# A hybrid streaming-encoder layer on one core: gates in order, a product moved, x on another queue, new planned transfer times

## The chip, the cores and the metric

One core of a Trainium2 chip runs the whole layer. The time is the device time of one execution, in microseconds (us). The engines are TensorE (PE; PEld are its weight loads), VectorE (DVE), ScalarE (ACT), GpSimd (POOL) and SyncE (SP), which only issues transfers. ScalarE and GpSimd issue transfers too.

## The reference, cut to what matters

```python
def hybrid_layer(x, norm_g, w_in, b_f, b_gate, qk_norm_g, rel_bias, w_up, w_out):
    b, s, _ = x.shape                                   # 1, 512, 2048
    hn = rmsnorm(x, norm_g)
    proj = jnp.einsum('bsd,dc->bsc', hn, w_in)
    br = proj[..., :QKVG_COLS].reshape(b, s, N_BRANCH, 4, BRANCH_W)
    f_logit = proj[..., QKVG_COLS:QKVG_COLS + N_HEADS] + b_f
    gates = jax.nn.sigmoid(proj[..., QKVG_COLS + N_HEADS:] + b_gate).reshape(b, s, N_BRANCH, D_MODEL)
    qa = rmsnorm(to_heads(br[:, :, 0, 0]), qk_norm_g[0])
    ...
    ya = forgetting_attention(qa, ka, to_heads(br[:, :, 0, 2]), f_logit)     # A: bias from a cumulative sum
    ...
    yb = chunked_relpos_attention(qb, kb, to_heads(br[:, :, 1, 2]), rel_bias) # B: learned relative bias
    yc = stick_breaking_attention(to_heads(br[:, :, 2, 0]), to_heads(br[:, :, 2, 1]),
                                  to_heads(br[:, :, 2, 2]))                   # C
    ys = jnp.stack([from_heads(ya), from_heads(yb), from_heads(yc)], axis=2)
    ys = ys * jax.nn.silu(br[:, :, :, 3])
    up = jnp.einsum('bsnw,nwd->bsnd', ys, w_up)
    merged = jnp.sum(gates * up, axis=2)
    return x + jnp.einsum('bsd,de->bse', merged, w_out)
```

Three branches of four heads of width 128 each; 512 tokens, all in float32. Nearly all of the arithmetic is in three products: the input projection (2048 to 12,292 columns), the up-projection of each branch (512 to 2048) and the output projection (2048 to 2048).

## The kernel before, in words

**Precision.** Every float32 operand is split into a high part and a rest, both in fp32r: hi is a copy by ScalarE, the rest a subtraction by VectorE. A product then takes three matmuls: hi x hi, hi x rest and rest x hi. For weights these are the tiles raw (as it lands), wh (L366, ScalarE) and wl (L371, VectorE). All matmuls of the large products stand on one helper line, L265. Eight raw buffers, three wh and two wl rotate.

**Work units.** The stream of work on TensorE is a list, units. A unit is one raw tile of weights, 128 x 1024, and twelve matmuls of 512 columns; its wh and wl are prepared two units ahead. The input projection and the output projection are cut by Strassen's scheme into tasks of seven products of four units each, (p, c) with p = 1 to 7 and c = 0 to 3. Products 1, 2 and 4 need one block of weights, a plain load by SyncE (L277). Products 5 and 7 need the sum of two blocks: a plain load, and then an accumulating transfer issued by GpSimd (L281) when the first has landed. Products 6 and 3 take 5's raw tile, to which VectorE adds the raw tile of 1 and then of 2 (L574). The results of a task are collected by Strassen.after: 5 and 1 are copied from their accumulators by ScalarE (L643), 6 and the others are added by VectorE (L652 on). There are four accumulators acc and four banks att for attention, transposes and, in one task, product 6.

**Stages.** First x is scaled and split while its sixteen blocks land (prep_x, L434 to L445); 42 matmuls on an identity matrix run on TensorE before the first real one (L417). Then twelve tasks, one per head: the C heads, the B heads, the A heads; the merge-gate logits gl and the branch inputs y are stored in memory and loaded again. The attention of a head is laid between the units of the next task. Then 24 units of the up-projection in twelve groups, (g, b) for four column groups g and three branches b: a group fills four accumulators, one for each of four token blocks tb, and VectorE multiplies each by a gate tile sg (L1251), to which ScalarE has applied the sigmoid (L1235, gates_of). From merged come the transposed operands m, their differences and splits (L256, L250), and then two output tasks, out_task(0) and out_task(1), whose results get x added and are stored.

**What sets the order.** The order of TensorE, ScalarE and VectorE is fixed while the kernel is written, by a planner (class Flow). Every piece of work is a generator that yields what it needs: an event, a buffer from a Slots pool, or an engine with a cost in us and a due time. Flow.run takes the piece that can start earliest by its own clocks, and among those the one due first. It reckons with planned landing times: landing for plain loads, add_up for accumulating ones, both on a common line. On the chip, the instructions of an engine run in the planned order, each waiting on what it really needs. SyncE's and GpSimd's queues follow the order in which the planner reaches the loads.

```python
    PLAIN = [(p, c) for p in (5, 1, 6, 7, 4, 2, 3) for c in range(CH)]
```

is the usual order of products.

## Time and profile before

| what | before |
|---|---|
| median of 3 runs | 1318.59 us (1318.33 to 1319.23) |
| the profiled execution | 1318.87 us, span 1317.2 us |
| TensorE busy | 1306.8 us, 99% of the span |
| VectorE, ScalarE, GpSimd busy | 1023.2, 751.5, 91.2 us |
| read and written | 266.03 MB, mean 202 GB/s |

In a timeline row stand the start, the length, the engine, the line, the operation, output and input, how many alike are joined in the row and, in brackets, how long the engine was idle ahead of it and what it waited for. In the chain of waits stand only the start, the length and what ran or was waited for. The row of a window begins with its length and the busy time of TensorE; in parentheses stand the numbers of instructions. The granted clock is 1.00 in all the stretches used.

### The profile page before, as it was taken

Reading aid. Unit: us, or ns where it says so; the run is one execution under the profiler, and the core shown is the slowest. Engines: PE = TensorE matmul, PEld = TensorE weight load, DVE = VectorE, ACT = ScalarE, POOL = GpSimd, SP = SyncE. Lnnn points to the kernel's source line nnn. Section 1 sums busy time; section 2 is a strip of 40 time slices with the busy share of each in tenths; the row PEclk is TensorE's granted clock in tenths of the full one; section 3 lists DMA queues with packets and bytes.
Section 4 is the critical chain, followed back from the end, with each engine's and each line's share of the span. In section 5 each row is a group of like instructions: output and inputs, shape, how many; then the busy total and the mean of one; then the engine's idle time right before and its main releaser. Section 6 shows DMA issues by size and latency. Waiting matters only on the chain.

```text
span 1317.2 us, 17191 instructions
## 1 busy us (share of the span) xinstructions
PE 1306.8 (99%) x6034; PEld 1078.7 (82%) x6034; DVE 1023.2 (78%) x1420; ACT 751.5 (57%) x1271; POOL 91.2 (7%) x115
## 2 busy tenths in 40 slices
PE   9999999999999999999999999999999999999998
PEld 7788888888888888888888888888887788878787
DVE  5877787887878777687776877778789668798667
ACT  7655464564557656566466654667568555454342
POOL 0000001110011100111011110110000000000110
PEclk9999999999999999999999999999999999999999
DMA  9755677866778757777577775777776656648883
GB/s 358 218 139 147 182 209 190 231 176 178 207 196 231 197 166 232 176 225 205 170 226 176 224 208 168 224 176 224 220 250 197 235 192 208 161 97 249 245 240 128
DMA packets 89063, 266.03 MB, mean 202 GB/s; under 512 B 11264, under 2 KB 11264, under 8 KB 88976
## 3 DMA queue, kind: packets, MB, share of 16 engines
q1 hardware_dynamic: 71552, 206.16, 46.5%
q0 software_dynamic: 14976, 54.53, 23.1%
q10 hardware_dynamic: 2448, 4.24, 0.8%
q8 instruction: 47, 0.77, 0.2%
q14 instruction: 40, 0.33, 0.1%
HBM read 245.19 MB, written 19.70 MB: 201 GB/s over the span
## 4 chain that ended last, share of the span: by engine, by line
PE 96%; DMA 2%; DVE 1%; ACT 1%; issue 0%; SPq 0%; ACTq 0%; POOLq 0%; DVEq 0%
PE acc L265 89%; DMA raw<-in_w_out 2%; PE att L801 1%; PE att L926 1%; PE att L260 1%; PE att L261 1%; PE att L262 1%; PE att L1016 1%; PE att L1015 1%; PE att L1285 1%; PE att L1014 1%; PE att L265 1%; ACT sg L1235 0%; DVE wl L371 0%; PE att L1118 0%; DMA x<-in_xT 0%
## 5 line engine op out<-in xcount | busy, mean ns | idle before, releaser
L371 DVE TENSOR_TENSOR wl<-raw,wh 128x1024 fp32r<-128x1024 f32 (+1 forms) x405 | 493.5, 1220 | 208.1 <-PE acc L265 116.1
L366 ACT ACTIVATE wh<-raw 128x1024 fp32r<-128x1024 f32 (+1 forms) x405 | 426.0, 1054 | 365.8 <-PE acc L265 276.3
L265 PE MATMUL acc<-wh,x 128*128 128x512 f32 x1664 | 429.8, 392 | 0.1
L265 PEld LDWEIGHTS acc<-wh,x 128*128 128x128 f32 x1664 | 308.7, 188 | 64.7 <-ACT t L246 0.9
L265 PE MATMUL acc<-wh,t 128*128 128x512 f32 x1056 | 272.6, 391 | 0.0
L265 PE MATMUL acc<-wl,x 128*128 128x512 f32 x832 | 229.8, 390 | 0.0
L265 PEld LDWEIGHTS acc<-wh,t 128*128 128x128 f32 x1056 | 196.7, 188 | 40.2
L265 PEld LDWEIGHTS acc<-wl,x 128*128 128x128 f32 x832 | 155.9, 188 | 33.1 <-DVE wl L371 0.4
L265 PE MATMUL acc<-wl,t 128*128 128x512 f32 x528 | 149.3, 390 | 0.0
L281 POOL DMA_DIRECT2D raw<-in_w_col x88 | 76.0, 864 | 877.5 <-ACT wh L366 195.3
L574 DVE TENSOR_TENSOR raw<-raw,raw 128x1024 f32<-128x1024 f32 x104 | 126.7, 1218 | 0.0
L265 PEld LDWEIGHTS acc<-wl,t 128*128 128x128 f32 x528 | 98.4, 188 | 19.6
L265 PE MATMUL acc<-wh,m 128*128 128x512 f32 x416 | 105.1, 390 | 1.9 <-ACT wh L366 1.9
L265 PE MATMUL acc<-wh,y 128*128 128x512 f32 x384 | 103.7, 391 | 1.3 <-DVE sg L1251 1.3
L265 PEld LDWEIGHTS acc<-wh,m 128*128 128x128 f32 x416 | 77.9, 188 | 18.8 <-ACT wh L366 2.7
L265 PEld LDWEIGHTS acc<-wh,y 128*128 128x128 f32 x384 | 71.7, 188 | 16.8 <-DVE sg L1251 2.2
L265 PE MATMUL acc<-wl,y 128*128 128x512 f32 x192 | 59.7, 391 | 0.0
L265 PE MATMUL acc<-wl,m 128*128 128x512 f32 x208 | 58.1, 390 | 0.1
L246 ACT ACTIVATE ah<-att 128x512 fp32r<-128x512 f32 (+3 forms) x48 | 21.0, 437 | 48.2 <-PE att L926 48.2
L265 PEld LDWEIGHTS acc<-wl,m 128*128 128x128 f32 x208 | 38.9, 188 | 8.5 <-DVE wl L371 0.5
L250 DVE TENSOR_TENSOR al<-att,ah 128x512 fp32r<-128x512 f32 (+3 forms) x48 | 23.5, 489 | 25.5 <-ACT ah L246 24.8
L265 PEld LDWEIGHTS acc<-wl,y 128*128 128x128 f32 x192 | 35.7, 188 | 7.2
(179 smaller groups left out, 1114.3 us busy)
## 6 DMA issues: line engine op xcount, KB each, us to landing
raw<-in_w_col SPq DMA_DIRECT2D x235, 512.0 KB, 4.6
raw<-in_w_col POOLq DMA_DIRECT2D x88, 512.0 KB, 7.9
raw<-in_w_out SPq DMA_DIRECT2D x40, 512.0 KB, 3.9
raw<-in_w_up SPq DMA_DIRECT2D x24, 512.0 KB, 3.6
sg<-gl SPq DMA_DIRECT2D x48, 256.0 KB, 4.6
raw<-in_w_out POOLq DMA_DIRECT2D x16, 512.0 KB, 6.2
gl<-u SPq DMA_DIRECT2D x22, 256.0 KB, 9.8
gl<-s SPq DMA_DIRECT2D x22, 256.0 KB, 5.2
```

What stands on the lines that cost most here:

```text
L246: nc.scalar.activation(hi, src, AF.Copy)
L250: nc.vector.tensor_sub(lo, src, f(hi))
L260: nc.tensor.matmul(ps, lh, rh, start=start, stop=False, skip_group_check=more)
L261: nc.tensor.matmul(ps, lh, rl, start=False, stop=False, skip_group_check=more)
L262: nc.tensor.matmul(ps, ll, rh, start=False, stop=stop, skip_group_check=more)
L265: nc.tensor.matmul(ps, w, x, start=start, stop=stop, skip_group_check=more)
L281: nc.gpsimd.dma_start(to, src, accum_op=ALU.add)
L366: nc.scalar.activation(u.hi, u.raw, AF.Copy)
L371: nc.vector.tensor_sub(u.lo, u.raw, f(u.hi))
L574: nc.vector.tensor_add(to.raw, to.raw, self.raw)
L801: nc.tensor.transpose(ps[:, blk(tb)], self.c[tb][:, blk(r)], identf)
L926: nc.tensor.transpose(ps[:, blk(i)], self.p[i][:, blk(j)], identf)
```

## The change

Seven parts:

1. The warm-up has 36 matmuls in place of 42, on a tile of ones that VectorE sets first, in a bank of its own. It no longer uses the identity, which GpSimd and VectorE make.
2. The planner's time of an accumulating transfer: it takes 250 KB/us of the common line, does not hold the line until its first half has landed, and lands 6.5 us later (it took 170 KB/us, waited, and landed 2.5 us later).
3. The constants are loaded by SyncE, ahead of everything, in place of ScalarE's queue; the first block of x is loaded by ScalarE's queue in place of SyncE's third place. The planner's clock begins at 4.0 in place of 5.0.
4. Buffers for wl are taken in the order of the units. The first unit's wh is made by VectorE, not ScalarE.
5. The first four blocks of x, not the first two, take the path that scales and copies in one ScalarE instruction; their plain scaling is due at 24.0.
6. The gates of the first group (g = 0, b = 0) are all asked for at one unit, so that they come ahead of the gates of later groups.
7. out_task(0) takes products 5 and 1 for all four columns before 6 (6 came after each pair of columns), and 6 uses acc banks. out_task(1) begins with product 1, then 5.

```diff
--- before.py
+++ after.py
@@ -29,7 +29,7 @@
 HS = S // 2
 EPS = 1e-6
 NEG = -1e30
-WARM = 42
+WARM = 36
 SCALE = HD ** -0.5
 LA = 2
 
@@ -279,8 +279,8 @@
 
     def add_up(to, src, ready, kb):
         nc.gpsimd.dma_start(to, src, accum_op=ALU.add)
-        line[1] = max(line[1], ready + 1.0) + kb / 170.0
-        return Event(line[1] + 2.5)
+        line[1] += kb / 250.0
+        return Event(max(line[1], ready) + 6.5)
 
     def stored(slots, n, kb):
 
@@ -289,12 +289,16 @@
 
     nc.scalar.preload_act_table_set("natural_log_exp_and_others")
     small_in = cp.tile([P, consts.shape[1]], F32, name="small_in")
-    nc.scalar.dma_start(small_in, consts)
+    nc.sync.dma_start(small_in, consts)
+    x_first = tp.tile([P, S], F32, tag="t2", name=nm("x"))
+    nc.scalar.dma_start(x_first, xT[0])
     gn = small_in[:, 0:KT]
     gqk = small_in[:, KT:KT + 4]
     bfc = small_in[:, KT + 4:KT + 5]
     wf = small_in[:, KT + 5:].rearrange("p (k h) -> p k h", h=NH)
 
+    oneb = cp.tile([P, P], BF16, name="oneb")
+    nc.vector.memset(oneb, 1.0)
     epsc = cp.tile([P, 1], F32, name="epsc")
     nc.gpsimd.memset(epsc, EPS)
     nhepsc = cp.tile([P, 1], F32, name="nhepsc")
@@ -343,6 +347,7 @@
 
 
         def __init__(self, mms, after=None, shape=(2, S), srcs=()):
+            self.took, self.prev = Event(), None
             self.shape, self.mms, self.after, self.srcs = list(shape), mms, after, srcs
             self.ready_hi, self.ready, self.there, self.raw = Event(), Event(), Event(), None
 
@@ -362,10 +367,17 @@
         n = u.shape[0] * S
         u.hi = wp.tile([P] + u.shape, F32R, tag="wh", name=nm("wh"), bufs=LA + 1)
         yield u.there
-        yield ACT, act_us(n)
-        nc.scalar.activation(u.hi, u.raw, AF.Copy)
+        if u is units[0]:
+            yield DVE, dve_us(n)
+            nc.vector.tensor_copy(u.hi, u.raw)
+        else:
+            yield ACT, act_us(n)
+            nc.scalar.activation(u.hi, u.raw, AF.Copy)
         set_(u.ready_hi)
+        if u.prev is not None:
+            yield u.prev.took
         yield wls, 1
+        set_(u.took)
         u.lo = wp.tile([P] + u.shape, F32R, tag="wl", name=nm("wl"), bufs=LA)
         yield DVE, dve_us(n)
         nc.vector.tensor_sub(u.lo, u.raw, f(u.hi))
@@ -413,8 +425,9 @@
     first_ps = att()
     atts.free.pop()
     nc.vector.memset(first_ps, 0.0)
+    early_ps = att()
     for _ in range(WARM):
-        nc.tensor.matmul(first_ps[:, :P], identb, identb, start=True, stop=True)
+        nc.tensor.matmul(early_ps[:, :P], oneb, oneb, start=True, stop=True)
     xps.free.clear()
 
 
@@ -428,15 +441,17 @@
         due = (5.0 + 3.2 * kt,)
         yield x_in[kt]
         x = xraw[kt]
-        if kt < 2:
+        if kt < 4:
             g = gn[:, kt:kt + 1]
             yield (ACT, act_us(S), *due)
             nc.scalar.activation(xs[kt].hi, two(x), AF.Copy, scale=g)
             set_(raw_hi[kt])
+            if kt == 0:
+                yield units[0].ready_hi
             yield (DVE, dve_us(S), *due)
             nc.vector.scalar_tensor_tensor(xs[kt].lo, two(x), g, f(xs[kt].hi), op0=ALU.mult, op1=ALU.subtract)
             set_(raw_ev[kt])
-            yield (DVE, 0.5, due[0] + 5.0)
+            yield (DVE, 0.5, 24.0)
             nc.vector.tensor_scalar_mul(x, x, g)
             set_(scaled[kt])
             return
@@ -1348,7 +1363,7 @@
     for g in (0, 2, 1, 3):
         for b in range(NB):
             for tb in range(QB):
-                at(len(units) - 3 + tb // 2, lambda n=(C, B, A)[b], g=g, tb=tb: gates_of(n, g, tb))
+                at(len(units) - (3 - tb // 2 if g or b else 2), lambda n=(C, B, A)[b], g=g, tb=tb: gates_of(n, g, tb))
             units.extend(up_units(g, b))
         for i in range(QB):
             at(len(units) - 1, lambda g=g, i=i: turned_m(g, i))
@@ -1376,11 +1391,10 @@
         def src(m, half, c):
             return w_out[2 * i + m, CH * half + c]
 
-        order, other = PLAIN, ()
+        order, other = PLAIN[CH:2 * CH] + PLAIN[:CH] + PLAIN[2 * CH:], ()
         if i == 0:
-            order = [(p, c) for cs in ((0, 1), (2, 3)) for p in (5, 1, 6) for c in cs]
-            order += PLAIN[3 * CH:]
-            other = (6,)
+            order = [(p, c) for cs in ((0, 1), (2, 3)) for p in (5, 1) for c in cs]
+            order += PLAIN[2 * CH:]
         return Strassen(src, mops, done, order, other, rest).units
 
     for i in range(2):
@@ -1390,6 +1404,9 @@
     def loads():
         def x(kt):
             yield t2s, 1
+            if kt == 0:
+                xraw[0], x_in[0].t = x_first, 3.6
+                return
             xraw[kt] = t2("x")
             x_in[kt].t = fetch(xraw[kt], xT[kt], 0.0, 256).t
 
@@ -1412,6 +1429,9 @@
         for u in units[9:]:
             yield from u.load()
 
+    for u, v in zip(units, units[1:]):
+        v.prev = u
+
     def stream():
         for i, u in enumerate(units):
             for g, slack in side.pop(i, ()):
@@ -1426,7 +1446,7 @@
                 spawn(u.after(), 0.0, flow.fin)
 
     line[0] = 0.8
-    flow.fin = 5.0
+    flow.fin = 4.0
     spawn(loads(), 0.0, 0.0)
     for kt in range(KT):
         spawn(prep_x(kt), 5.0)
```

Three places where the planned order moves.

**SyncE, then VectorE, at the first up-projection group.** sg is a gate tile, gl the logits in memory; in the rows of before, sg_9142 and sg_9167 are the gates of token blocks 0 and 1 of the first group, sg_9123 and sg_9125 of blocks 2 and 3. SyncE before:

```order
L277 DMA sg_9123<-gl_6773 128x512
L277 DMA sg_9125<-gl_6794 128x512
L277 DMA sg_9127<-gl_3786 128x512
L277 DMA sg_9129<-gl_3813 128x512
L277 DMA sg_9131<-gl_3889 128x512
L277 DMA sg_9133<-gl_3910 128x512
L277 DMA sg_9137<-gl_1042 128x512
L277 DMA sg_9139<-gl_1052 128x512
L277 DMA sg_9142<-gl_6670 128x512
L277 DMA raw_9148<-in_w_up 128x1024
L277 DMA sg_9167<-gl_6697 128x512
```

and with the change:

```order
L277 DMA sg_9120<-gl_6667 128x512
L277 DMA sg_9122<-gl_6694 128x512
L277 DMA sg_9124<-gl_6770 128x512
L277 DMA sg_9126<-gl_6791 128x512
L277 DMA sg_9128<-gl_3783 128x512
```

VectorE before:

```order
L1023 TENSOR_TENSOR y_8961<-y_8961,att_9116 128x512
L1251 TENSOR_TENSOR sg_9123<-acc_9087,sg_9123 128x512
L250 TENSOR_TENSOR y_9136<-y_8961,y_9136 128x2x256
L1251 TENSOR_TENSOR sg_9125<-acc_9101,sg_9125 128x512
L371 TENSOR_TENSOR wl_9208<-raw_8888,wh_9141 128x1024
L1251 TENSOR_TENSOR sg_9142<-acc_9055,sg_9142 128x512
L1251 TENSOR_TENSOR sg_9167<-acc_9076,sg_9167 128x512
L371 TENSOR_TENSOR wl_9255<-raw_8915,wh_9206 128x1024
```

and with the change, where sg_9120 to sg_9126 are the four gates of the first group:

```order
L250 TENSOR_TENSOR al_9102<-att_9164,ah_9101 128x128
L1266 TENSOR_TENSOR sg_9120<-acc_9048,sg_9120 128x512
L1038 TENSOR_TENSOR y_8944<-y_8944,att_9111 128x512
L1266 TENSOR_TENSOR sg_9122<-acc_9064,sg_9122 128x512
L1266 TENSOR_TENSOR sg_9124<-acc_9081,sg_9124 128x512
L250 TENSOR_TENSOR y_9137<-y_8944,y_9137 128x2x256
L1266 TENSOR_TENSOR sg_9126<-acc_9099,sg_9126 128x512
L383 TENSOR_TENSOR wl_9205<-raw_8871,wh_9140 128x1024
```

The four gates of the first group are now loaded first, in the order of their token blocks, and VectorE multiplies them in that order ahead of two weight splits.

**VectorE in the first output task.** The raw tiles are the weights of the products; mt, mu and m are operands. Before:

```order
L371 TENSOR_TENSOR wl_10354<-raw_10016,wh_10326 128x1024
L256 SCALAR_TENSOR_TENSOR mt_10330<-mt_10330,m_10064 128x256
L371 TENSOR_TENSOR wl_10380<-raw_9876,wh_10351 128x1024
L256 SCALAR_TENSOR_TENSOR mu_10322<-mt_10321,m_10319 128x256
L250 TENSOR_TENSOR m_1992_10366<-mt_10310,m_1992_10366 128x2x256
L574 TENSOR_TENSOR raw_9937<-raw_9937,raw_10016 128x1024
L250 TENSOR_TENSOR m_1994_10372<-m_10299,m_1994_10372 128x2x256
L256 SCALAR_TENSOR_TENSOR mu_10322<-mt_10330,m_10328 128x256
L371 TENSOR_TENSOR wl_10407<-raw_10085,wh_10397 128x1024
L250 TENSOR_TENSOR m_2000_10401<-mt_10321,m_2000_10401 128x2x256
L250 TENSOR_TENSOR m_2001_10405<-m_10308,m_2001_10405 128x2x256
L371 TENSOR_TENSOR wl_10427<-raw_9937,wh_10379 128x1024
```

With the change:

```order
L256 SCALAR_TENSOR_TENSOR mt_10327<-mt_10327,m_10078 128x256
L250 TENSOR_TENSOR m_1993_10364<-mt_10307,m_1993_10364 128x2x256
L383 TENSOR_TENSOR wl_10378<-raw_10083,wh_10348 128x1024
L256 SCALAR_TENSOR_TENSOR mu_10319<-mt_10318,m_10316 128x256
L250 TENSOR_TENSOR m_1995_10369<-m_10296,m_1995_10369 128x2x256
L589 TENSOR_TENSOR raw_9934<-raw_9934,raw_10014 128x1024
L256 SCALAR_TENSOR_TENSOR mu_10319<-mt_10327,m_10325 128x256
L383 TENSOR_TENSOR wl_10399<-raw_10132,wh_10377 128x1024
L250 TENSOR_TENSOR m_1998_10391<-m_10305,m_1998_10391 128x2x256
L250 TENSOR_TENSOR m_2001_10406<-mt_10318,m_2001_10406 128x2x256
L250 TENSOR_TENSOR m_1994_10368<-mu_10299,m_1994_10368 128x256
L383 TENSOR_TENSOR wl_10423<-raw_10168,wh_10398 128x1024
```

Before, wl_10407 is that of unit (5,2) and wl_10427 that of (6,1), whose raw_9937 is summed by L574 six rows earlier. With the change the split at this place (wl_10399) is that of (5,3), wl_10423 that of (1,2), and the summed tiles are split later.

**VectorE in the first B head.** tb is the bias tile that a transfer brings, p the probabilities; L1068 became L1083, L881 became L896, L371 became L383. Before:

```order
L1068 SCALAR_TENSOR_TENSOR s_3493<-s_3493,rstd,bg_3642 128x512
L371 TENSOR_TENSOR wl_3915<-raw_3709,wh_3892 128x1024
L371 TENSOR_TENSOR wl_3944<-raw_3734,wh_3914 128x1024
L371 TENSOR_TENSOR wl_3946<-raw_3760,wh_3929 128x1024
L574 TENSOR_TENSOR raw_3657<-raw_3657,raw_3760 128x1024
L371 TENSOR_TENSOR wl_3972<-raw_3803,wh_3942 128x1024
L574 TENSOR_TENSOR raw_3687<-raw_3687,raw_3803 128x1024
L881 MEMSET tb_3852 64x64
```

With the change:

```order
L383 TENSOR_TENSOR wl_3892<-raw_3684,wh_3869 128x1024
L1083 SCALAR_TENSOR_TENSOR s_3497<-s_3497,rstd,bg_3639 128x512
L896 MEMSET tb_3849 64x64
L383 TENSOR_TENSOR wl_3912<-raw_3706,wh_3889 128x1024
L917 ISA p_3917,mx_3927<-att_3923,tb_3849 128x128
L917 ISA mx_3927 128x1
L919 TENSOR_SCALAR mx_3927<-mx_3927 128x1
L917 ISA p_3918,mx_3933<-att_3929,tb_3849 128x256
```

The memset on tb stood behind four weight splits and two sums, and now stands ahead of all of them, with the first row of the softmax close behind.

## The prediction

> **What bounds the kernel now.** I read the page first, then the chain of waits from end to start, then the timeline wherever the chain leaves TensorE. The page's busy times and its chain shares:
>
> ```profile
> PE 1306.8 (99%) x6034; PEld 1078.7 (82%) x6034; DVE 1023.2 (78%) x1420; ACT 751.5 (57%) x1271; POOL 91.2 (7%) x115
> ...
> PE 96%; DMA 2%; DVE 1%; ACT 1%; issue 0%; SPq 0%; ACTq 0%; POOLq 0%; DVEq 0%
> ```
>
> TensorE is the bound and its work stays the same, so the change can only win back time in which TensorE stands. The chain's end, two transfers of weights and then TensorE:
>
> ```profile
> 1222.27 9.44 DMA raw<-in_w_out
> ...
> 1232.26 11.08 DMA raw<-in_w_out
> ...
> 1245.81 67.40 PE acc L265 x296
> ```
>
> The last stretch is unbroken and gives the pitch: 67.40 / 296 = 0.2277 us a matmul, 2.73 us for a unit of 12. From the start of one row of matmuls to the start of a later one, whatever exceeds 0.2277 us for each matmul between them is a stall; I use that below, because the idle times alone leave out the slow refill after a wait. From the up-projection on, the chain leaves TensorE for long at three places, each quoted with its term below. Before them lie the heads (160 to 985 us, by stretch; first TensorE's busy time and its matmuls):
>
> ```profile
> 160.00:985.00 825.00, 825.00 (x3819) 684.68 (x3818) 649.48 (x866) 491.42 (x845) 69.02 (x80) 1.00 0.73 203
> ```
>
> TensorE is busy for 825.00 of 825.00 us. There is nothing to gain in the heads, only something to lose.
>
> **Start** (parts 1, 3, 4 and 5 of the change: fewer warm-up matmuls without the wait for the identity, x and the constants on exchanged queues, the first wh on VectorE). Timeline, then two rows of busy time by stretch (TensorE, its loads, VectorE, ScalarE, GpSimd, clock, DMA share, GB/s):
>
> ```profile
> 1.93 4.31 PE L417 MATMUL att<-identb 128*128 128x128 bf16 x42 [1.93 <-DVE identb L310]
> 5.00 0.72 ACT L434 ACTIVATE x<-x,small_in 128x512 fp32r<-128x512 f32 x1 [2.90 <-DMA x<-in_xT]
> 5.62 0.61 ACT L366 ACTIVATE wh<-raw 128x512 fp32r<-128x512 f32 x1
> 6.29 2.11 PE L265 MATMUL acc<-wh,x 128*128 128x512 f32 x8
> ...
> 21.63 1.06 ACT L366 ACTIVATE wh<-raw 128x1024 fp32r<-128x1024 f32 x1 [0.22 <-DMA raw<-in_w_col]
> 22.75 3.50 PEld L265 LDWEIGHTS acc<-wh,x 128*128 128x128 f32 x16 [0.16 <-ACT wh L366]
> ```
>
> ```profile
> 1.90:5.60 3.70, 3.67 (x35) 3.68 (x36) 0.60 (x4) 0.80 (x2) 0.13 (x1) 1.00 1.00 286
> 12.00:22.00 10.00, 10.00 (x46) 8.11 (x45) 6.38 (x11) 8.00 (x21) 0.00 (x0) 1.00 1.04 391
> ```
>
> x lands at 5.00; ScalarE then makes x (0.72) and wh (0.61) one after the other. With wh on VectorE the second falls away, about 0.6 us; x leaves its queue earlier by about 0.4 us, but the first weights and constants change places. First product: estimated 5.2 to 5.9 us instead of 6.29, so 0.4 to 1.1 earlier. How much stays? At 21.63 ScalarE waits for a landing of weights, and TensorE waits for that copy at 22.75. The stretch before moves 391 GB/s with the DMA engines busy throughout, and the change takes no byte from it. So the lead is mostly given back at 22.75. I take **0.2 us**, from -0.3 (the swap of queues delays the weights) to 0.7 (the lead survives).
>
> The warm-up is cut to 36 matmuls. 35 of them take 3.70 us at the slow pace, 0.106 us each, so 36 last 3.8 us, about as long as the slow pace lasts now. The Trainium skill, "TensorE: Matmul & The Clock Gate", Part 1: The HAM clock gate, says that the budget is about 3.4 us of time and not a number of matmuls, with a turning point that varies by 500 ns because the window runs freely. The trace agrees with the length (3.7 us); by the rule, half a microsecond of first products may run at half pace, a loss estimated at 0.25 us, which lies inside the bounds above.
>
> The same holds for x on ScalarE's queue: the row above shows full engines. The Trainium skill, "DMA: Bandwidth & Descriptors", Queues, rings and completion order, says that a queue has rings of its own on the same sixteen engines, which take turns among queues. By that rule another queue brings an earlier issue and no bandwidth, so the start's term would be 0; the saturated stretch above agrees.
>
> **Gates in order** (part 6). The first up-projection group:
>
> ```profile
> 1028.56 0.61 PE L265 MATMUL acc<-wl,y 128*128 128x512 f32 x2
> 1029.20 1.19 PE L265 MATMUL acc<-wh,y 128*128 128x512 f32 x4
> 1029.71 3.22 ACT L1235 ACTIVATE sg<-sg 128x512 f32<-128x512 f32 x6
> 1030.23 0.63 PE L265 MATMUL acc<-wl,y 128*128 128x512 f32 x2
> 1031.40 1.29 DVE L1251 TENSOR_TENSOR sg<-acc,sg 128x512 f32<-128x512 f32 x2 [1.12 <-ACT sg L1235]
> 1032.14 1.20 PE L265 MATMUL acc<-wh,y 128*128 128x512 f32 x4 [1.29 <-DVE sg L1251]
> 1033.18 0.62 PE L265 MATMUL acc<-wl,y 128*128 128x512 f32 x2
> ```
>
> From 1028.56 to 1033.18 are 4.62 us for 2 + 4 + 2 + 4 matmuls, 12 x 0.2277 = 2.73: a stall of 1.89 us. Two of the four accumulators wait to be multiplied by gates whose sigmoids come behind eight others on ScalarE. In the new order the four gates of this group are first on SyncE, ScalarE and VectorE. The last accumulator is then multiplied when its own products end; the later sigmoids, 3.22 / 6 = 0.54 us each, keep ahead of the groups that need them, one every 5.5 us. What can remain: the last head now ends about 1 us later in VectorE's order, and the table load with it. I take **1.8 us**; bounds 1.4 (the later head) and 1.89.
>
> **Sixth product moved** (first half of part 7).
>
> ```profile
> 1169.57 1.22 DVE L371 TENSOR_TENSOR wl<-raw,wh 128x1024 fp32r<-128x1024 f32 x1
> 1169.99 2.07 PE L265 MATMUL att<-wh,m 128*128 128x512 f32 x8
> 1173.18 1.20 PE L265 MATMUL att<-wl,m 128*128 128x512 f32 x4 [1.12 <-DVE wl L371]
> 1174.22 1.98 PE L265 MATMUL acc<-wh,m 128*128 128x512 f32 x8
> ```
>
> 1169.99 to 1174.22 are 4.23 us for 12 matmuls: 4.23 - 2.73 = 1.50 us. VectorE is late: it splits the operands of m at the same time, the weights of (6,1) must be summed before they can be split, and the split of (5,2), a unit later, has run ahead of it (the row at 1169.57). In the new order the sixth product comes behind all eight units of 5 and 1; here stand (5,2) and (5,3), whose weights VectorE need not sum. The sums stay in its queue, but no split waits for one, and one split of 1.22 us less stands ahead of the sixth unit's. That unit, (5,3), now takes the place of (5,2) on VectorE and ends at 1169.57 + 1.22 = 1170.79 or a little earlier. As the last unit of its product it goes by token block, so its split is wanted after four matmuls, at 1169.99 + 4 x 0.2277 = 1170.90: 0.1 to 0.15 us to spare, and the later ones have more. The sixth product's two banks now come from the accumulators of 5, copied off by ScalarE in 2 x 0.61 us (the row at 5.62 has that shape) two units, 5.5 us, before they are wanted; without that cover it would cost 1.2. I take **1.35 us**; bounds 0.8 (the thin split is 0.7 late) and 1.50.
>
> **Second output task begins with its first product** (second half of part 7).
>
> ```profile
> 1232.26 0.86 POOL L281 DMA_DIRECT2D raw<-in_w_out  x1 [5.37 <-DMA raw<-in_w_out]
> 1238.60 1.07 PE L265 MATMUL acc<-wl,m 128*128 128x512 f32 x4
> 1240.10 2.12 PE L265 MATMUL acc<-wh,m 128*128 128x512 f32 x8 [0.43 <-ACT wh L366]
> 1242.05 1.07 PE L265 MATMUL acc<-wl,m 128*128 128x512 f32 x4
> 1244.55 1.19 PE L265 MATMUL acc<-wh,m 128*128 128x512 f32 x4 [1.44 <-ACT wh L366]
> 1245.81 0.74 PE L265 MATMUL acc<-wl,m 128*128 128x512 f32 x2
> 1246.38 0.85 PE L265 MATMUL acc<-wh,m 128*128 128x512 f32 x3
> ```
>
> 1238.60 to 1246.38 are 7.78 us for 4 + 8 + 4 + 4 + 2 = 22 matmuls, 5.01: a stall of 2.77 us. The fifth product's weights need two transfers in a row, a plain load and an accumulating one, 9.44 and 11.08 us in the chain, the second issued only at 1232.26. The first product needs one load. In the new order four plain loads go out first and are used for four units, 10.9 us; the four accumulated ones, issued in the same place after them, are wanted 10.9 us later. Four loads of 512 KB more ahead of them take about 2048 / 391 = 5.2 us of the stream at the pace quoted above, half of the cover. I take **2.7 us**, bounds 2.2 and 2.77. The work after the last product is not touched.
>
> **Other planned transfer times** (part 2) remove no instruction. They let the planner put scores and transposes 8 to 11 us earlier in nearly every head, in orders that the engines must keep. By tile: the bias tile tb of the B heads (issue, VectorE's first touch, landing after issue), then the row cr that is scanned in the A heads, then VectorE's timeline in the first B head:
>
> ```profile
> L277 SPq DMA_DIRECT2D tb<-in_rel x4: 433/450/480, 421.5 to 669.8; - x4
> L881 DVE MEMSET tb<- x4: 112/112/112, 443.6 to 691.8; 64x64 f32 x4
> DMA to landing us min/median/max: 11.2/11.7/12.1
> ```
>
> ```profile
> L874 DVE TENSOR_TENSOR_SCAN cr<-cr x4: 1216/1220/1220, 774.4 to 993.5; 128x512 f32<-128x512 f32 x4
> DMA to landing us min/median/max: 11.6/11.9/12.1
> ```
>
> ```profile
> 432.09 0.75 DVE L1068 SCALAR_TENSOR_TENSOR s<-s,rstd,bg 128x512 f32<-128x512 f32 x1
> 433.11 1.23 DVE L371 TENSOR_TENSOR wl<-raw,wh 128x1024 fp32r<-128x1024 f32 x1 [0.27 <-issue]
> 435.83 1.23 DVE L371 TENSOR_TENSOR wl<-raw,wh 128x1024 fp32r<-128x1024 f32 x1 [1.50 <-PE acc L265]
> ```
>
> Now the memset comes 10 us after the landing (421.5 + 12.1 = 433.6, memset at 443.6). In the new order it stands right behind the instruction that ends at 432.84, so VectorE will wait 0.8 us for tb with weight splits queued behind it, and TensorE waits for those. The next split has 1.50 us of idle ahead of it, so 0.8 us is covered: 0 for the four B heads. In the A heads the scan (1.22 us) is moved ahead of four splits in the same way; my walk, with landings 11.6 to 12.1 us after the issue, makes one split in one head 0.3 to 0.4 us late. I take **-0.4 us** in all, from 0 to -1.5 (each of the four A heads like the worst).
>
> **Sum.** 0.2 + 1.8 + 1.35 + 2.7 - 0.4 = 5.65 us off the profiled execution's 1318.87 (span 1317.2 and 1.7 around it): 1313.2; the median of the runs, 1318.59, lies 0.28 lower, so **1313.0 us**. The terms' own ends, 6.86 and 2.6 us off the median, give 1311.7 to 1316.0.
>
> **Rivals.** (a) *Only partly*: one late stall stays or reappears. For it: the margin of 0.1 us in the first output task, and VectorE without a pause there. Against: the order takes a split out of its way. If the first output task gains nothing, 1313.0 + 1.35 = 1314.4. (b) *The heads eat it*: TensorE works in order, so a transpose placed 10 us early waits on its own exponentials. My walk of a C head leaves 0.8 us of margin; if it is missed by 0.9 in four C heads, 3.6 us go: 1316.6, no change that can be told. Against: TensorE is now busy for the whole of 825 us, with no such wait. (c) *Slower, by tb and cr*: VectorE stands in front of its splits for a late landing in four B and three A heads. In a B head the stall is 0.8 + d - 1.5 us when the landing comes d later than 12.1 us. It decides when the seven together lose more than the 5.65 gained and 2.6 besides, 1.2 us a head, d = 1.9. At 1.4 a head, 9.8 us stand in place of the 0.4: 1313.0 + 9.4 = 1322.4. For it: the planner no longer counts accumulating transfers against the loads, so it reckons with landings that are too early. Against: landings vary by only 11.2 to 12.1, and their issue order hardly changes. (d) *The change doesn't do what it says*: an order written by a planner could move the gates and yet stall elsewhere in the same group; that is counted in (a).
>
> **How the numbers follow.** Forecast 0.62, (a) with (d) 0.18, (b) 0.12, (c) 0.08. 0.2% of 1318.59 is 2.64 us, about what a measurement of this kernel can tell from no change: faster means under 1315.95, slower over 1321.23. Faster 0.62 + 0.18 = 0.80, same 0.12, slower 0.08. The range runs from a little under the forecast's own low end to a little into (b), 1311.0 to 1316.3; it leaves out (c) and the slower half of (b), 0.14, and the forecast's rare best.
>
> **What would show it.** Start: first product at 5.2 to 5.9 us, and a wait for weights near 22.7 as before; if that wait moves with the start, the lead survives. Gates: no matmul row in the first group with idle time ended by VectorE's sg. First output task: no idle in the stretch of products 5 and 1. Second: no wait for ScalarE's wh in its first eight units, the accumulated weights landing before they are wanted. Heads: VectorE idle ended by a DMA ahead of the tb memset, about 0.8 us, and TensorE still busy for the whole stretch; idle of TensorE in each head proves (b), if ended by att or p, or (c), if ended by wl. The forecast is wrong if the heads lose more than 3 us, or if two of the three late stalls stay.

## The result, and the profile after

The changed kernel takes 1311.95 us (median of 6 runs, 1311.58 to 1312.61), the kernel before 1318.76 us on the same chip (6 runs, 1318.26 to 1319.23): a ratio of 0.9948 with a 95% interval of 0.9938 to 0.9959. Run once more, again beside the kernel before, it takes 1312.13 us against 1318.73. The forecast was 1313.0, in a range of 1311.0 to 1316.3. The profiled execution is 6.65 us shorter (1318.87 to 1312.22), its span 6.7 (1317.2 to 1310.5); the sum had said 5.65.

The page of the changed kernel, busy times and chain shares:

```profile
PE 1305.2 (100%) x6028; PEld 1079.2 (82%) x6028; DVE 1026.3 (78%) x1422; ACT 755.6 (58%) x1270; POOL 91.3 (7%) x115
...
PE 99%; DMA 1%; SPq 0%; ACT 0%; DVE 0%; issue 0%
```

TensorE has 99% of the chain where it had 96%. The end of the chain of waits, changed kernel:

```profile
1024.95 26.37 PE acc L265 x116
...
1156.12 150.39 PE acc L265 x663
1306.53 0.69 DVE s L703
```

From 1156.12 on it never leaves TensorE: 150.39 / 663 = 0.2268 us a matmul through both output tasks. The stretches of the three stalls, by window (length, TensorE's busy time, its weight loads, VectorE, ScalarE, GpSimd, then clock, DMA share and GB/s):

```profile
1021.00:1034.00 13.00, 13.00 (x64) 10.95 (x63) 7.19 (x11) 10.93 (x19) 0.00 (x0) 1.00 1.04 387
1158.00:1180.00 22.00, 22.00 (x98) 18.09 (x97) 22.00 (x33) 15.78 (x24) 1.72 (x2) 1.00 0.51 130
1220.00:1247.00 27.00, 27.00 (x121) 22.37 (x120) 17.93 (x17) 12.04 (x13) 4.31 (x5) 1.00 0.92 249
```

TensorE is busy in every microsecond of them. To say where the 6.64 us between first and last row of the two traces went, I took the same large matmul in both, counted from the first one (5328 of them in each kernel), and compared its start. The column on the left is the forecast of that term; positive is time won.

| stretch, us | forecast | won |
|---|---|---|
| start, to 41 | 0.2 | 0.04 |
| heads but the last, 41 to 977 | -0.4 (all heads) | -0.28 |
| last head, 977 to 1027 | in the row above | 0.78 |
| first up-projection group, 1027 to 1049 | 1.8 | 1.92 |
| first output task, 1049 to 1187 | 1.35 | 1.43 |
| its rest, 1187 to 1230 | 0 | 0.00 |
| start of the second, 1230 to 1252 | 2.7 | 2.81 |
| after 1252 | 0 | -0.06 |

The one row that the forecast has nothing for is the last head. It was in the profile before, in the chain, and I had read past it: my window for the heads ended at 985 us, and the first stall that I looked at lay behind 1021. Chain of the kernel before, two sets of four transposes:

```profile
996.96 0.97 PE att L801 x4
997.93 3.21 PE acc L265 x14
1001.14 0.44 PE att L801 x4
```

Timeline of the kernel before at the first of them:

```profile
996.28 0.68 ACT L793 ACTIVATE w<-w,norms 128x128 f32<-128x128 f32 x2
996.80 0.55 PE L801 MATMUL att<-identf,w 128*128 128x128 f32 x2
996.87 0.68 ACT L793 ACTIVATE v<-v,norms 128x128 f32<-128x128 f32 x2
997.31 0.62 PE L801 MATMUL att<-identf,v 128*128 128x128 f32 x2
```

Four transposes take 0.44 us at every other place of this chain and 0.97 here: ScalarE makes their operands one after the other, some 0.3 us apart, and TensorE has come too early. No idle time is marked: TensorE counts as busy there. The chain of the changed kernel at this place:

```profile
994.42 3.67 PE acc L265 x16
998.09 0.44 PE att L816 x4
```

They now take 0.44. The other 0.24 us of the 0.78 is a weight split that was late at 1004; this one is marked, on the weight loads of the kernel before:

```profile
1004.76 0.76 PEld L265 LDWEIGHTS acc<-wl,x 128*128 128x128 f32 x4 [0.39 <-DVE wl L371]
```

### The profile page after: what moved, and what is told of

Its sections match the earlier page's. It is cut to its first block, busy times and chain, and to the rows that moved or that the text cites. A ratio compares the mean times of both kernels' runs of the same rounds, so it can differ in the third digit from the quotient of the medians.

```text
span 1310.5 us, 17137 instructions
## 1 busy us (share of the span) xinstructions
PE 1305.2 (100%) x6028; PEld 1079.2 (82%) x6028; DVE 1026.3 (78%) x1422; ACT 755.6 (58%) x1270; POOL 91.3 (7%) x115
## 4 chain that ended last, share of the span: by engine, by line
PE 99%; DMA 1%; SPq 0%; ACT 0%; DVE 0%; issue 0%
PE acc L265 92%; PE att L816 1%; PE att L941 1%; PE att L1031 1%; PE att L1030 1%; PE att L261 1%; PE att L262 1%; PE att L260 1%; PE att L1029 1%; PE att L1300 1%; DMA raw<-in_w_col 1%; PE att L1133 0%; SPq L277 0%; PE att L913 0%; ACT wh L375 0%; DVE s L703 0%
## 5 line engine op out<-in xcount | busy, mean ns | idle before, releaser
L383 DVE TENSOR_TENSOR wl<-raw,wh 128x1024 fp32r<-128x1024 f32 (+1 forms) x405 | 493.0, 1219 | 195.1 <-PE acc L265 139.8
L265 PE MATMUL acc<-wh,x 128*128 128x512 f32 x1664 | 434.3, 393 | 0.2
L265 PE MATMUL acc<-wh,m 128*128 128x512 f32 x448 | 112.9, 389 | 0.0
L265 PEld LDWEIGHTS acc<-wh,m 128*128 128x128 f32 x448 | 84.1, 188 | 17.4
L265 PE MATMUL acc<-wl,m 128*128 128x512 f32 x224 | 62.5, 390 | 0.0
L265 PEld LDWEIGHTS acc<-wl,m 128*128 128x128 f32 x224 | 41.9, 188 | 8.8 <-DVE wl L383 0.2
L1266 DVE TENSOR_TENSOR sg<-acc,sg 128x512 f32<-128x512 f32 x48 | 32.8, 689 | 5.0 <-PE acc L265 2.6
```

Source lines behind the costliest of these rows:

```text
L265: nc.tensor.matmul(ps, w, x, start=start, stop=stop, skip_group_check=more)
L383: nc.vector.tensor_sub(u.lo, u.raw, f(u.hi))
L1266: nc.vector.tensor_mul(t, ps[tb], t)
```

## The experiments

Times are medians, beside the kernel before on the same chip. The stretches are compared with the changed kernel by the same matmuls as above, start apart, because the start varies by itself (last section).

**Gates in the old order.**

```diff
-at(len(units) - (3 - tb // 2 if g or b else 2), ...)
+at(len(units) - 3 + tb // 2, ...)
```

> The changed kernel with part 6 alone undone (the first group's gates asked for in two pairs, as before). Theory, the stall of the first up-projection group came from the order of the gates: TensorE waits again for VectorE's sg there, 1.9 us, and the median is 1313.9 instead of 1311.95. Rival, the other planned transfer times had already moved the last head and the gates: no more than 0.5 us comes back, median 1312.0 to 1312.5.

Measured 1314.36 us against 1318.80 (ratio 0.9968, 0.9956 to 0.9980). In the first group 2.33 us come back, in no other stretch more than 0.02. Timeline of this run:

```profile
1028.84 3.74 ACT L1250 ACTIVATE sg<-sg 128x512 f32<-128x512 f32 x7
1028.85 1.19 PE L265 MATMUL acc<-wh,y 128*128 128x512 f32 x4 [0.31 <-DVE sg L1266]
1031.05 1.29 DVE L1266 TENSOR_TENSOR sg<-acc,sg 128x512 f32<-128x512 f32 x2 [1.12 <-ACT sg L1250]
1031.79 1.19 PE L265 MATMUL acc<-wh,y 128*128 128x512 f32 x4 [1.29 <-DVE sg L1266]
```

It is the old wait to a hundredth (1.12 and 1.29 us), with 0.31 us added to it. The theory stands, and the rival falls.

**First output task in the old order.**

```diff
-order = [(p, c) for cs in ((0, 1), (2, 3)) for p in (5, 1) for c in cs]
-order += PLAIN[2 * CH:]
+order = [(p, c) for cs in ((0, 1), (2, 3)) for p in (5, 1, 6) for c in cs]
+order += PLAIN[3 * CH:]
+other = (6,)
```

> The changed kernel with the first output task's order undone (6 after each pair of columns, in attention banks), but with wl buffers still taken in the order of the units. Theory, the sum that the sixth product's weights need makes VectorE late: 1.4 us come back, median 1313.4, with TensorE waiting for wl in the task's sixth unit. Rival, the harm was the split of (5,2) that had run ahead of that of (6,1): with wl in the order of units at most 0.3 us comes back, median 1312.0 to 1312.3.

Measured 1312.73 us against 1318.80 (0.9955, 0.9940 to 0.9970). At the sixth unit only 0.31 us comes back, as the rival says, and 0.45 later, at 1196, where another split is late; the median, with both in it, lies between the two numbers. So the sum was not the cause of most of the 1.43 us. Timeline of this run:

```profile
1167.29 2.07 PE L265 MATMUL att<-wh,m 128*128 128x512 f32 x8
1168.08 2.35 DVE L383 TENSOR_TENSOR wl<-raw,wh 128x1024 fp32r<-128x1024 f32 x2
1169.35 1.19 PE L265 MATMUL att<-wl,m 128*128 128x512 f32 x4
```

VectorE makes two splits in a row from 1168.08, and the first is the one that is due: (6,1), summed and all, is split before (5,2).

**Second output task beginning with its fifth product.**

```diff
-order, other = PLAIN[CH:2 * CH] + PLAIN[:CH] + PLAIN[2 * CH:], ()
+order, other = PLAIN, ()
```

> The changed kernel with the second output task beginning with its fifth product again. Theory, two transfers in a row for each of the fifth product's weights: TensorE waits 2.8 us in the first four units, median 1314.75, with ScalarE's wh waiting for a transfer. Rival, part of the stall came from the loads of the first task, whose order is changed too: 1.5 us or less, median at most 1313.5.

Measured 1313.39 us against 1318.80 (0.9958, 0.9944 to 0.9971). 1.35 us comes back, less than half of 2.81. Timeline of this run:

```profile
1224.20 0.86 POOL L281 DMA_DIRECT2D raw<-in_w_out  x1 [0.92 <-DMA raw<-in_w_out]
1237.68 2.96 ACT L375 ACTIVATE wh<-raw 128x1024 fp32r<-128x1024 f32 x3 [4.19 <-DMA raw<-in_w_out]
1238.80 1.21 PE L265 MATMUL acc<-wh,m 128*128 128x512 f32 x4 [0.71 <-ACT wh L375]
```

The fourth accumulating transfer goes out at 1224.20, where it went out at 1232.26 in the kernel before. TensorE is 4.30 us ahead of that kernel by then, so the other parts bring this load 3.8 us forward against the work, and only one unit out of four still waits. The rival is right on the size.

**Old planned times.**

```diff
-line[1] += kb / 250.0
-return Event(max(line[1], ready) + 6.5)
+line[1] = max(line[1], ready + 1.0) + kb / 170.0
+return Event(line[1] + 2.5)
```

> The changed kernel with the planned times of accumulating transfers undone (part 2). Theory after comparing the two traces: the heads lose 0.28 us by part 2 (more and shorter stretches on TensorE) and the last A head gains 0.78 by it (transposes that no longer wait 0.53 us, a weight split no longer 0.24 late), so undoing it costs 0.5 us: median 1312.45. Rival, as forecast: part 2 only costs, 0.3 to 0.4 us, and the last head's gain comes from other parts: median 1311.6.

Measured 1313.61 us against 1318.80 (0.9960, 0.9947 to 0.9972), more than either number. By stretch: the heads give 0.29 back and the last head costs 0.79, as the theory had it, but 0.87 us more is lost at the start of the second output task, where neither theory had anything. Timeline of this run there:

```profile
1248.80 1.06 ACT L375 ACTIVATE wh<-raw 128x1024 fp32r<-128x1024 f32 x1 [1.61 <-PE acc L265]
1249.89 2.36 DVE L383 TENSOR_TENSOR wl<-raw,wh 128x1024 fp32r<-128x1024 f32 x2 [2.90 <-ACT wh L375]
1249.91 1.19 PE L265 MATMUL acc<-wh,m 128*128 128x512 f32 x4 [0.24 <-ACT wh L375]
```

ScalarE stands 1.61 us waiting for TensorE before it may make a wh that TensorE wants next. Its planned order says why:

```
ACTIVATE wh_11035<-raw_10849      (6,0)
ACTIVATE wh_11000<-raw_10877      (5,2)
ACTIVATE wh_11056<-raw_10863      (6,1)
ACTIVATE wh_11022<-raw_10893      (5,3)
```

Under the old times the planner believed the accumulated weights of (5,2) and (5,3) to land later than the sums of (6,0) and (6,1) to be ready, and gave two of the three wh buffers to units that come later.

**The same with wh in the order of units.**

```diff
 yield u.there
+if u.prev is not None:
+    yield u.prev.ready_hi
```

> The changed kernel with the planned times of accumulating transfers undone, as in the earlier run, and wh made in the order of the units as well. In that run TensorE lost 0.87 us at 1249 to 1251 us; ScalarE's order there has wh of the sixth product's first two units ahead of wh of (5,2) and (5,3). Theory, that order is the whole of the 0.87: it is gone, and the end comes 0.87 us earlier than in that run (span 1310.8 with the same start). Rival, the accumulated weights themselves are late under the old costs: 0.5 us or more stays at 1249.

Measured 1312.73 us against 1318.73 (0.9952, 0.9937 to 0.9967). The 0.87 us is gone; the stretch from 1230 to 1252 equals the changed kernel's to 0.01. The chain of this run, and below it that of the run with old times alone, over the same window:

```profile
1243.82 10.20 PE acc L265 x45
```

```profile
1243.78 5.00 PE acc L265 x22
1248.78 0.02 issue
1248.80 1.07 ACT wh L375
1249.87 0.02 issue
1249.89 1.24 DVE wl L383
```

The span is 1311.1 instead of the expected 1310.8: at 41 us this execution stood 0.40 us behind that of the run with old times alone, of which the last head gave back 0.15.

**Only wl in the order of units**, added to the kernel before.

```diff
+if u.prev is not None:
+    yield u.prev.took
 yield wls, 1
+set_(u.took)
```

> The kernel before with one thing added: wl buffers are taken in the order of the units (the half of part 4 that I had costed at nothing). Theory after the run that undid the first output task's order (only 0.31 us came back at the sixth unit, not 1.43): the split of (5,2) running ahead of that of (6,1) was most of that stall, so this alone takes 1.1 us off there, and the median is 1.1 to 1.5 us below the kernel before. Rival, the order of splits matters only together with the new order of products: 0.3 us or less.

Measured 1318.04 us against 1318.73 (0.9994, 0.9985 to 1.0003): by the times it can't be told from no change. By the traces 1.13 of the 1.43 us at the sixth unit is gone, and 0.21 at the second output task. Timeline of this run:

```profile
1170.65 2.35 DVE L375 TENSOR_TENSOR wl<-raw,wh 128x1024 fp32r<-128x1024 f32 x2
1171.92 1.20 PE L265 MATMUL att<-wl,m 128*128 128x512 f32 x4
```

TensorE gets the split at 1171.92 where it got it at 1173.18. The theory stands at its place, while the median moved by 0.69 us, short of the 1.1 to 1.5 expected.

**Parts 6 and 7 alone**, with wl in the order of units, on the kernel before (the three diffs above, the other way round).

> The kernel before with parts 6 and 7 alone, and with wl buffers taken in the order of units, which their order needs. Theory, the three stalls are independent of the rest: 1.92 + 1.43 + 2.81 = 6.16 us off 1318.76, median 1312.6, so that parts 1 to 5 without that are worth 0.6 us. Rival, the three terms need the new planned times: less than 5 us off, over 1313.8.

Measured 1313.78 us against 1318.32 (0.9965, 0.9952 to 0.9977), 4.54 us: by the median the rival's side. By the traces the truth lies between the two: 1.92, 1.45 and 1.94 us in the three stretches, 5.31 for the theory's 6.16; the second output task keeps the same 0.87 us as under the old times. Of the three stalls only that one needs the new times.

**The start undone** (warm-up, queues, first wh, direct path of x).

```diff
-WARM = 36
+WARM = 42
-nc.sync.dma_start(small_in, consts)
-nc.scalar.dma_start(x_first, xT[0])
+nc.scalar.dma_start(small_in, consts)
...
-        if kt < 4:
+        if kt < 2:
```

> The changed kernel with the start undone: constants and x on their former queues, 42 warm-up matmuls on the identity, the first wh on ScalarE, two blocks of x on the direct path. Theory, the lead of 1.2 us at the first product is given back by 35 us: median 1312.0, within 0.1 of the changed kernel, with the first product at 6.3 us. Rival, the start is worth 0.4 us or more: median over 1312.35.

Measured 1312.75 us against 1318.32 (0.9953, 0.9940 to 0.9967), by the trace 0.48 us behind the changed kernel at 41 us. Seven executions with the new start, all with the same instructions to that point, stood there between 0.41 us ahead of the changed kernel's profiled one and 0.37 behind, 0.07 ahead in the mean; four with the old start between 0.06 ahead and 0.48 behind, 0.19 behind in the mean. That is 0.26 us in favour of the new start, with ranges that overlap. The median is on the rival's side, but this execution was also an unlucky one: its first eight products took 2.63 us, those of the kernel before, with the same warm-up, 1.95 (last section). So what the start is worth is not settled. This run loses 0.21 us more in the last head, at 997 us, where its planned order brings a weight split late.

**Twelve warm-up matmuls.**

```diff
-WARM = 36
+WARM = 12
```

> The changed kernel with 12 warm-up matmuls instead of 36. Theory, TensorE runs at half its pace until it has worked for about 3.7 us: the first real products take 0.43 us each instead of 0.23, and as only 0.2 us of lead is left at the fourth unit, the end is 0.5 to 1.5 us later, median 1312.5 to 1313.5. Rival, the first units wait for transfers anyway and hide it: the same within 0.2 us.

Measured 1312.82 us against 1318.32 (0.9956, 0.9943 to 0.9970). By the trace 1.11 us behind at 41 us, and to the end. TensorE in this run:

```profile
1.13 1.46 PE L430 MATMUL att<-oneb 128*128 128x128 bf16 x12 [1.13 <-DVE oneb L301]
5.12 3.75 PE L265 MATMUL acc<-wh,x 128*128 128x512 f32 x8 [2.52 <-DVE wh L372]
8.66 1.91 PE L265 MATMUL acc<-wl,x 128*128 128x512 f32 x4
```

The first eight products take 8.66 - 5.12 = 3.54 us, 0.44 each, twice their pitch; the transfers don't hide it. The theory stands in its outcome; the slow pace lasts longer than its 3.7 us, for 13 products, 5.5 us from the first of them.

**x in its natural layout loaded later; and the constants on ScalarE's queue besides.** The first moves the 16 loads of xn behind the first blocks of x and weights and the squares' due time from 12 to 38 us; the second adds:

```diff
-nc.sync.dma_start(small_in, consts)
+nc.scalar.dma_start(small_in, consts)
```

> The changed kernel with the 16 loads of the untransposed x (256 KB each, wanted only for the norm) moved behind the blocks of x and weights that the first units need, and ScalarE's squares of them due 26 us later. Theory, the stream of transfers is what gives the lead back: with 4 MB less ahead of it, TensorE keeps most of the 1.46 us that it stands between 5 and 41 us, median 1310.7. Rival, ScalarE is the limit there, or the transfers in flight share the engines whatever comes behind them: 0.3 us or less is gained, or the squares collide with later work, median 1311.7 or more.

> The changed kernel with the loads of the untransposed x moved back, as in the earlier run, and the constants on ScalarE's queue ahead of the first x, so that SyncE's first transfer is the first weights. Theory, transfers share one stream, and their order sets the start: the second block of x and its weights land 0.3 us earlier, the end is 0.2 to 0.4 us earlier than with the loads moved alone (span 1309.1 to 1309.3), and 1.0 to 1.4 us before the changed kernel on this chip. Rival, the constants now hold up the first x on their own queue: the first product 0.3 us later, and nothing or less gained against the earlier run.

> The changed kernel itself once more, beside the next one on the same chip. Theory: five executions whose first 40 us are the same program reached unit 12 at 41.25 us less 0 to 0.43, so the start varies by some 0.4 us from execution to execution, and the median is 1311.5 to 1312.3 with the kernel before at 1318.5.

Measured, each against the kernel before beside it: 1311.27 against 1318.32 (0.9947, 0.9934 to 0.9959); 1312.04 against 1318.73 (0.9955, 0.9942 to 0.9967); the changed kernel again 1312.13 against 1318.73 (0.9949, 0.9936 to 0.9961). In the traces the first stands 1.00 us ahead of the changed kernel at 41 us, beyond the 0.41 that the start reaches by itself, the second 0.61, although its first product starts at 5.95 us. Both keep the lead to the end. The seven executions with xn in its place lose 0.21 to 0.36 us of their lead near 35 us; these two lose none there. The medians don't show a gain: 7.05, 6.69 and 6.60 us off the kernel before. So a later xn probably helps by some tenths of a microsecond, and that it beats the changed kernel isn't shown; its 1311.27 lies between the theory's 1310.7 and the rival's 1311.7. With the constants on ScalarE's queue besides, the rival stands: the first product comes 0.98 us later, and nothing is gained on the first of the two runs. The changed kernel again came out inside the forecast of 1311.5 to 1312.3.

## Why the prediction was right, and where it was wrong

**Sign, range and size** hold: 6.8 us by the medians for a forecast of 5.6. Most of the miss is one term: the heads were sized at -0.4 and came to +0.50, because the last head's stall was not in my list. I had listed the stalls from the idle marks and from the pitch between two large matmuls: no window of mine covered 985 to 1021 us, and for transposes that wait for their operands neither sign would have helped. The -0.4 was wrong in its mechanism too: it stood for a weight split that comes late in an A head, and between 41 and 977 us no wait for a split is marked on the weight loads of the changed kernel.

**Gates**: the mechanism and the size (1.8 for 1.92). Undone alone it costs 2.33, more than 1.89, probably because the last head ends earlier by the new times and leaves more for the gates to hold up; no run separates that.

**Sixth product moved**: the size was right (1.35 for 1.43) for the wrong step; whatever ends that stall gives this size, so the number is no support for the step. I wrote that VectorE is late because of the sum and that the new order of products takes a split out of its way. What ran ahead was cured by the half of part 4 that takes wl in the order of units, which I had costed at nothing: 1.13 us by itself, and 0.31 for the new order of products. The margin that I worked out for the split of (5,3), 0.1 to 0.15 us, is there. Changed kernel:

```profile
1167.11 1.22 DVE L383 TENSOR_TENSOR wl<-raw,wh 128x1024 fp32r<-128x1024 f32 x1
1167.53 1.07 PE L265 MATMUL acc<-wh,m 128*128 128x512 f32 x4
1168.43 0.68 PE L265 MATMUL acc<-wl,m 128*128 128x512 f32 x2
```

It ends at 1168.33 and TensorE takes it at 1168.43, 0.10 us later.

**Second output task**: the size again (2.7 for 2.81), with a share given to the wrong part. The order of products alone, undone, brings back 1.35; with old planned times 0.87 stays in spite of the new order. I had costed part 2 only by what it moves in the heads. Whether the 3.8 us by which the last load comes forward with the old order of products is due to the first task's order or to the new times was not separated.

**Other planned times**: the forecast of a wait on tb is right and costs nothing. Changed kernel, timeline in the first B head:

```profile
431.97 0.75 DVE L1083 SCALAR_TENSOR_TENSOR s<-s,rstd,bg 128x512 f32<-128x512 f32 x1
433.17 0.11 DVE L896 MEMSET tb<- 64x64 f32 x1 [0.46 <-DMA tb<-in_rel]
```

The waits of VectorE on that tile over the four heads, in us, times and the longest:

```profile
DVE tb L896 <- DMA tb<-in_rel: 1.9, 3, 0.9
```

The longest is 0.9 for a forecast of 0.8, and no split came late to TensorE by it. The loss of 0.28 us in the heads is spread: in the whole trace there are 73 places, up from 67, where a large matmul follows another 60 to 120 ns later than the pitch. In all, part 2 is a gain: undoing it costs 0.79 - 0.29 + 0.87 = 1.37 us.

**Start**: the first product comes at 5.06 us, a little before my 5.2 to 5.9, and the lead of 1.23 us is given back. In the profiled execution it goes at once and not at 22.75. Changed kernel:

```profile
5.06 2.49 PE L265 MATMUL acc<-wh,x 128*128 128x512 f32 x8
8.53 1.69 PEld L265 LDWEIGHTS acc<-wh,x 128*128 128x128 f32 x8 [0.49 <-ACT wh L375]
10.50 1.06 ACT L375 ACTIVATE wh<-raw 128x1024 fp32r<-128x1024 f32 x1 [0.58 <-DMA raw<-in_w_col]
11.62 0.53 PEld L265 LDWEIGHTS acc<-wh,x 128*128 128x128 f32 x3 [0.50 <-ACT wh L375]
```

By 12.65 us 0.12 of the lead is left. That was chance: here the second weights land at 10.48 us, in the six other executions with this start at 9.52 to 10.22 (at 8.89 to 9.66 in the four with the old start). Those six still have 0.40 to 0.99 us of lead on the kernel before at 22.7 us and lose it later, near 28 and 35 us; at 41 us they stand between 0.45 ahead and 0.33 behind, so the 0.04 of the table neither bears out my 0.2 nor refutes it. What all eleven share is that later weights land no sooner with the new start: those on which the row at 10.50 waits, and those issued near 28 us, at 34.1 to 35.1 us with either start. An earlier issue on another queue brought the first product forward and no later landing. The Trainium skill, "DMA: Bandwidth & Descriptors", Queues, rings and completion order, says that each queue has rings of its own on the same sixteen engines; the landings agree.

**Rivals.** None came in the changed kernel. (b) had its place wrong: a transpose placed too early did stall TensorE, but in the kernel before, and the change mended it. In (c) the landings of tb stayed at 11.7 to 12.1 us, far from the 14 that it needed.

## What to carry to other kernels

With few buffers between engines that run in a fixed order, look first whether anything is made ahead of what is due next: two splits in the wrong order cost 1.13 us here, two copies 0.87, and it looked like late sums and late transfers. A planner's times decide such orders even where no engine or queue is short, so a wrong time for one kind of transfer shows up far from any transfer. And when terms of a sum come out right, undo the parts one by one before believing their causes; list the stalls by the pace of every kind of matmul, not by idle marks alone.

## What the runs showed of the hardware

The same instructions need not start alike. Seven executions with the same program up to 41 us differ by 0.78 us there. In the second run of the changed kernel a wait for a landing makes the difference:

```profile
27.00 1.06 ACT L375 ACTIVATE wh<-raw 128x1024 fp32r<-128x1024 f32 x1 [0.21 <-DMA raw<-in_w_col]
28.11 2.11 PE L265 MATMUL acc<-wh,x 128*128 128x512 f32 x8 [0.47 <-ACT wh L375]
```

Differences of a few tenths of a microsecond in the medians are therefore no evidence on a part of the change, while the stretches of the traces behind the start agree from run to run to about 0.02 us.

Some executions begin the real products at the slow pace, with 36 warm-up matmuls as with 42. The run with the old gates, whose start is that of the changed kernel, and below it the run with the start undone:

```profile
4.91 2.76 PE L265 MATMUL acc<-wh,x 128*128 128x512 f32 x8
7.51 1.08 PE L265 MATMUL acc<-wl,x 128*128 128x512 f32 x4
```

```profile
6.34 2.79 PE L265 MATMUL acc<-wh,x 128*128 128x512 f32 x8
8.97 1.07 PE L265 MATMUL acc<-wl,x 128*128 128x512 f32 x4
```

Their first eight take 2.60 and 2.63 us, where eight at the full pitch take 1.81; the first three of each run at the slow pace, two of these at 0.43 us, the pace of the run with 12 warm-up matmuls. The trace's record of the granted clock turns to full speed between 3.1 us (the changed kernel again) and 6.0 us (the start undone) after the first warm-up matmul, in the 13 traces with 36 or 42 of them. In the kernel before it was 3.8, and from that one execution I had taken the length of the slow pace. The Trainium skill, "TensorE: Matmul & The Clock Gate", Part 1: The HAM clock gate, speaks of a time that varies by about 500 ns because its window runs freely. The variation is there, but it is 2.9 us here, and the measurement decides: neither the 3.8 us that 36 matmuls last at the slow pace nor the 4.5 us of 42 are sure to be enough. The clock of 1.00 that the window view gives for 1.90 to 5.60 us is no evidence against this: the trace's record begins at 5.71 us, and the warm-up matmuls before it come every 0.107 us, those after it every 0.056.
